# One-layer decoder trunk on one core: the low parts of the MLP's and the last gate's weight chunks come from an accumulating transfer instead of a VectorE subtraction

## The chip, the cores and the metric

The kernel runs on one core of one Trainium2 chip. The metric is the device time of one execution in microseconds (us). The profile is of one execution, with times counted from the first instruction of the span. Engines are called by the profile's names: PE is TensorE (PEld its weight loads), DVE is VectorE, ACT is ScalarE, POOL is GpSimd, and SP is the engine whose queue issues most transfers.

## What is computed

One layer on a 512 x 1024 residual stream `x`, all in float32:

```
h = RMSNorm(x)
[conv_a | conv_b | q | k | v | pool | gates] = h @ W_in
mix = W_out( sum_b sigmoid(gate_b) * y_b ); x += RMSNorm(mix)     # y: conv, attention, pooling
x += RMSNorm( squared-ReLU MLP( RMSNorm(x) ) )                    # 1024 -> 4096 -> 1024
x += sigmoid(x @ W_pg) * (p @ W_pe)
```

The change touches the weights of the last two lines: the MLP's two matrices and the gate `W_pg`.

## The kernel before

**Products.** Activations lie with features on the 128 partitions and the 512 tokens along the free dimension. A float32 product is made of three fast ones: each operand is split into a high part `h`, rounded to the fast product's type, and an exact rest `l`, and `mm3` (lines 153 to 155 of the kernel's text) adds h·h, h·l and l·h in one PSUM bank. In the profile L153 and L155 read `wh` and `wl` against the high part of the moving operand, and L154 reads `wh` against its low part.

**Weights.** All matrices are packed into 142 chunks of 128 x 1024 floats (512 KB), in the order in which they are used. Chunks 62 to 69 are `W_out`, 70 to 133 the MLP in four quarters of the hidden width (eight chunks of its first matrix, then eight of its second), 134 to 141 the last gate. A chunk serves one output tile: 8 steps over the inner dimension (kt) of three products, 24 products in all. The class `Weights` loads a chunk on SP's queue into one of 3 raw buffers (L75), `split` (L86) makes the high part on ACT (L89, a cast) and the low part on DVE (L93, raw minus high), into one of 8 pairs of buffers in the part that matters here; `get` asks for chunks ahead, as far as buffers and `W.limit` allow. A pair comes free when PE has done the last product of the chunk that held it, eight chunks earlier.

**Order.** Each engine runs its own list in order. A scheduler makes the lists from the program's text by a model of times; in the stretches marked `manual_schedule` PE's own instructions keep the order of the text. `W.pin` with `keep_in_program_order` ties an instruction to its place behind the one that is written before it on the same engine: `side_by_side_halves` (L865) uses it for the four chunks (74 to 77, later 138 to 141) that it asks for after 15 steps of products.

**The two norms at the MLP's start.** `W_out`'s last five tiles and the MLP's first four (chunks 70 to 73, `side_by_side_halves`) are multiplied by halves of the tokens, so that the norm of one half runs while the other half is multiplied. For each half, `residual_half` (L842) lets PE sum squares (L210), DVE and POOL make the reciprocal root (L200, L202), PE spread it (L215) and ACT copy it to `mB` (L845). Then DVE scales the eight tiles `mix` (L850), POOL adds them to `x` (L851), and ACT and DVE split the scaled `x` into `xgh` and `xgl` (`mul_split`, L148 and L149), which are the operand of the MLP's first matrix. The sums of squares for the second norm (`x1sum`) are gathered on the way. Its reciprocal root, needed only after the first matrix, goes through DRAM: `rstd_dma` (L219) copies a row of sums (ACT, L223), and four transfers follow one another in POOL's queue: `d1` (L226), `c4` (L228), after a power on POOL `d2` (L230), and `rB` (L232). `hidden` (L892) needs `rB` to make the operand `sh`, `sl` of the second matrix. The same scheme by halves stands at the MLP's end, with `f`, `fsum`, `fB` and `x2h`, `x2l` in place of `mix`, `msum`, `mB`, `xgh` and `xgl`.

Of the kernel before, what the change touches and what calls it, by code (L numbers as in the profile page):

```python
# [13 lines left out]

# the work of the first half in order, by the letters of the table
ORDER = [dict(A="conv", Q="qk", V="v", P="pool", p="pool out", a="attention out", c="conv gates")[c]
         for c in "QAVPAAQQQppppcAaaaaccc"]
# shares of TensorE's time given to the background work during projections and gates
RATE_IN, RATE_GATE = 0.6, 0.907
# of the steps of background work, how many are taken from the first queue for one from the second  # L20
TURNS = 2
# steps to wait for the sums of a norm: a head's, the last head's, LayerNorm's
NORM_LAG, WAIT_SUB, WAIT_LN = 10, 4, 8
# start: tiles of x loaded before the second chunk; chunks split before x is normalized; normalized
# tiles of x before the next chunks; products that bring up the array's clock
X_BEFORE_W1, W_EARLY, XN_BEFORE_W3, XN_BEFORE_W4, N_WARM = 3, 2, 2, 7, 8
# products of a half before the other half's sums, and before they are spread; chunks split after that
PACE_SUM, PACE_SPREAD, W_AHEAD = 8, 15, 3
# output tiles multiplied side by side before those by halves
N_SIDE = 3  # L30
# slots: raw chunks, split chunks, activations, logits, tiles of norms, q and k
N_RAW, N_SPLIT, N_ACT, N_LOGIT, N_NORM, N_QK = 3, 3, 32, 6, 3, 10
TCARGS = dict(schedule_with_timeline_sim=True)
P = 128
# [10 lines left out]

# columns of the packed small parameters
G_PRE_MIX, G_POST_MIX, G_PRE_MLP, G_POST_MLP = 0, 8, 16, 24
# [9 lines left out]
class Weights:  # L57
    """Streams the packed weight chunks in order: a load and a split of each
    chunk into its rounded high part and the exact rest."""

# [25 lines left out]
    def split(self, c, sl=slice(0, 1024), parts="hl"):  # L86
        src, (wh, wl) = self.raw[c][:, sl], self.tiles[c]
        if "h" in parts:
            i = self.nc.scalar.copy(out=wh[:, sl], in_=src)  # L89
            if self.pin:  # L90
                self.tc.keep_in_program_order(i)
        if "l" in parts:
            i = self.nc.vector.tensor_tensor(out=wl[:, sl], in0=src, in1=wh[:, sl].bitcast(F32), op=ALU.subtract)  # L93
            if self.pin:
                self.tc.keep_in_program_order(i)
# [15 lines left out]
def block_kernel(ctx: ExitStack, tc: tile.TileContext, xT, pT, wts, pool_w, par, rel_bias, onehot, out):  # L111
# [15 lines left out]

    # tiles that wait for a long chain have slots of their own: slots of a tag are
    # given out in order, so they would hold up all that comes after them
    BUFS = {"a": N_ACT, "lg": N_LOGIT, "bias": 2, "norm": N_NORM}  # L130
# [15 lines left out]
    def mul_split(h, l, src, scale=1.0):  # L146
        """h + l = src * scale, h rounded to the fast product's operand."""
        nc.scalar.activation(out=h, in_=src, func=AF.Copy, scale=scale)  # L148
        nc.vector.scalar_tensor_tensor(out=l, in0=src, scalar=scale, in1=h.bitcast(F32),  # L149
                                       op0=ALU.mult, op1=ALU.subtract)  # L150
# [5 lines left out]

# [1 line left out]
    start = ExitStack()  # L158
# [28 lines left out]
    nc.vector.memset(neghalf, -0.5)  # L187
    # products whose result nobody reads, so that the array's clock is up when the data comes
    warm = bank("at")
# [5 lines left out]

# [1 line left out]
    def rstd_from(ssq, inv_n, n, name):  # L197
        """[P, n] sums -> (sum * inv_n + eps) ** -0.5"""
        c = small(n, name + "c")
        nc.vector.tensor_scalar(out=c, in0=ssq, scalar1=inv_n, scalar2=EPS, op0=ALU.mult, op1=ALU.add)  # L200
        r = small(n, name + "r")
        nc.gpsimd.tensor_tensor(out=r, in0=c, in1=neghalf[:, 0:n], op=ALU.pow)  # L202
        return r

    def rstd_steps(sq, lo, n, inv_n, got, tag="at"):
        """column sums of sq[:, lo:lo+128n] to rstd, the same on every partition, in PSUM: a step
        for the sums and one that spreads them and hands them to got"""
        b = bank(tag)
        for j in range(n):
            nc.tensor.matmul(out=b[:, j:j + 1], lhsT=sq[:, lo + j * P:lo + (j + 1) * P], rhs=ones_col,  # L210
                             start=True, stop=True)
        r = rstd_from(b[:, 0:n], inv_n, n, "pe")
        yield
        for j in range(n):
            nc.tensor.matmul(out=b[:, j * P:(j + 1) * P], lhsT=r[:, j:j + 1].to_broadcast([P, P]),  # L215
                             rhs=ident, start=True, stop=True)
        got(b[:, 0:n * P])
# [16 lines left out]

    # ---- background streams: steps for DVE between the products, each step
    # yielding its cost in us, or None when it can't go on yet ----
    class Stream:
# [3 lines left out]
        def step(self):  # L241
            """one step; its cost, or None when the stream is blocked or over"""
            try:
                return next(self.gen)
            except StopIteration:
                self.over = True
                return None
# [41 lines left out]

# [1 line left out]
    LEFT, RIGHT = slice(0, 512), slice(512, 1024)  # L291
# [73 lines left out]

# [1 line left out]
    lam_t = cp.tile([P, 8], F32, name="lam_t")  # L367
# [11 lines left out]

    # sigmoid(z) = (1 + tanh(z / 2)) / 2, so that one table serves exp and the gates;  # L380
    # the factor 1/2 goes where a scale is applied anyway
    nc.vector.tensor_scalar(out=pcol(DW_W, 4 * CW), in0=pcol(DW_W, 4 * CW), scalar1=0.5, scalar2=None, op0=ALU.mult)
# [9 lines left out]
    nc.sync.dma_start(out=rel_d, in_=rel_r)  # L392
    # row r of a head's bias is its row of distances moved by r
    rep_d = dr.tile([NH, P, 640], F32, name="rep_d")
# [3 lines left out]

# [1 line left out]
    def project(n, evac, side_by_side=False):  # L400
        """n output tiles of the combined projection"""
        bs = []
        if side_by_side:
            cs = [next_chunk() for _ in range(n)]
            bs = [bank() for _ in range(n)]
            for kt in range(KT):
                for (wh, wl), b in zip(cs, bs):
                    mm3(b, wh[:, kt * P:(kt + 1) * P], wl[:, kt * P:(kt + 1) * P], *xn[kt], kt == 0, kt == KT - 1)
        else:
            for _ in range(n):  # L410
                wh, wl = next_chunk()
                bs.append(bank())
                for kt in range(KT):
                    mm3(bs[-1], wh[:, kt * P:(kt + 1) * P], wl[:, kt * P:(kt + 1) * P], *xn[kt], kt == 0, kt == KT - 1)
                    tick(0.65 * RATE_IN)
        return evac(bs)
# [3 lines left out]
    def evac_qk(bs):  # L420
        """q and k of a head's two maps, stacked so that a product over 128 rows holds two of the
        three terms: high q twice against high and low k; and low q where the high k lies"""
        qb, kb = bs
# [25 lines left out]
    def attention():  # L449
# [37 lines left out]
        def transpose(i):  # L487
            # keys of all blocks up to this pair of query blocks on the partitions
            qb = i % 4
# [196 lines left out]

# [1 line left out]
    merged = [None] * KT  # L688
# [78 lines left out]

    # ---- output projection; its last tiles by token halves, so that the norm
    # of one half runs while the other half is multiplied ----
    x_t = []  # L770
# [13 lines left out]
    class Paced:  # L784
        """the steps of a norm, set between the products of the other half"""

# [14 lines left out]
    def split_output(src, evac, done):  # L801
        """8 output tiles of a product over 8 kt: some side by side, the others by halves."""
        W.limit = chunk[0] + KT + 3
# [38 lines left out]
    def residual_half(hf, src, ssum, rB, xs, use):  # L842
        """xs += src * rstd of the half, and what uses the sum"""
        sl = HALVES[hf]
# [18 lines left out]

# [1 line left out]
    def side_by_side_halves(src, done):  # L865
# [67 lines left out]

# [1 line left out]
    proj = []  # L935
# [36 lines left out]
def _layout(inp):  # L972
# [7 lines left out]
    def tiles(w):  # L980
        """[K, M] -> [M/128][128, K/128, 128]"""
        k, m = w.shape
# [89 lines left out]
```

## Time and profile before

| | |
|---|---|
| time, median of 3 runs | 867.05 us (865.79 to 867.57) |
| span of the profiled execution | 864.5 us |
| PE busy | 848.3 us (98%) |
| DVE busy | 512.3 us (59%) |
| ACT busy | 352.5 us (41%) |
| POOL busy | 50.4 us (6%) |
| moved by DMA | 89.38 MB, mean 103 GB/s |

The profiled execution's span is 2.55 us below the median of the three runs, which hold what lies around the span as well; a sum made on the trace is added to the median as it stands. Busy is the time in which an engine had an instruction under way; the rows below show single instructions, groups of them, or stretches of the span.

### The profile page before, as it was taken

What the parts mean: (1) busy time and instruction counts of PE and PEld (TensorE: products, weight loads), DVE (VectorE), ACT (ScalarE), POOL (GpSimd) and SP (SyncE); (2) the same over time, 40 slices, a digit from 0 to 9 for tenths busy, and PEclk for the clock granted to TensorE, in tenths of its full rate; (3) what the DMA queues carried; (4) which work ended last, traced back from release to release, by engine and by line L of the source; (5) the groups of instructions that cost most, each with busy time, mean ns of one, the idle gap of its engine ahead of it and who ended that gap; (6) DMA issues with size and microseconds to landing.
All of it is one profiled execution on the core that took longest, in us unless ns stands there. A gap on an engine that the chain in (4) does not pass through costs nothing.

```text
span 864.5 us, 10723 instructions
## 1 busy us (share of the span) xinstructions
PE 848.3 (98%) x4202; PEld 707.9 (82%) x4202; DVE 512.3 (59%) x803; ACT 352.5 (41%) x568; POOL 50.4 (6%) x85
## 2 busy tenths in 40 slices
PE   9979999999999999999999999999999999999998
PEld 6767888777778888888999778888888888889987
DVE  5749659965559996658368453344344434425682
ACT  6625435464443323553454354342124313425341
POOL 2100000010000000000033100000000000000420
PEclk9989999999999999999999999999999999999999
DMA  8353222121122222255201614222222222212311
GB/s 296 122 194 114 106 98 98 68 91 54 69 74 74 96 99 96 76 191 204 91 27 53 204 49 146 98 98 97 99 98 98 97 90 88 99 65 75 122 50 74
DMA packets 28127, 89.38 MB, mean 103 GB/s; under 512 B 3272, under 2 KB 3656, under 8 KB 28076
## 3 DMA queue, kind: packets, MB, share of 16 engines
q1 hardware_dynamic: 27260, 86.32, 28.6%
q0 software_dynamic: 816, 2.37, 0.7%
q8 instruction: 33, 0.54, 0.2%
q14 instruction: 18, 0.15, 0.1%
HBM read 84.47 MB, written 5.52 MB: 104 GB/s over the span
## 4 chain that ended last, share of the span: by engine, by line
PE 86%; DVE 5%; DMA 4%; issue 3%; ACT 1%; POOL 1%; SPq 0%; DVEq 0%; ACTq 0%; POOLq 0%
PE mm L153 19%; PE mm L155 19%; PE mm L154 19%; PE at L153 8%; PE at L154 8%; PE at L155 8%; DMA raw<-in_wts_dram 2%; DVE f L850 1%; PE at L462 1%; PE at L215 1%; POOL x L851 1%; PE at L210 1%; DVE mix L850 1%; PE at L460 1%; PE at L493 1%
## 5 line engine op out<-in xcount | busy, mean ns | idle before, releaser
L89 ACT CAST wh<-raw 128x1024 fp32r<-128x1024 f32 (+1 forms) x144 | 148.6, 1038 | 334.5 <-PE mm L154 151.0
L93 DVE TENSOR_TENSOR wl<-raw,wh 128x1024 fp32r<-128x1024 f32 (+1 forms) x144 | 173.4, 1209 | 104.6 <-ACT wh L89 104.3
L155 PE MATMUL mm<-xnh,wl 128*128 128x512 f32 x352 | 138.6, 394 | 0.1
L153 PE MATMUL mm<-xnh,wh 128*128 128x512 f32 x352 | 137.9, 394 | 0.0
L154 PE MATMUL mm<-xnl,wh 128*128 128x512 f32 x352 | 137.8, 392 | 0.0
L582 DVE SCALAR_TENSOR_TENSOR acc<-u,par_sb,acc 128x512 f32<-128x512 f32 x116 | 82.2, 748 | 0.1
L153 PEld LDWEIGHTS mm<-xnh,wh 128*128 128x128 f32 x352 | 66.1, 188 | 15.7 <-issue 1.0
L155 PEld LDWEIGHTS mm<-xnh,wl 128*128 128x128 f32 x352 | 66.1, 188 | 15.0 <-issue 0.8
L154 PEld LDWEIGHTS mm<-xnl,wh 128*128 128x128 f32 x352 | 66.1, 188 | 13.8 <-DVE xnl L149 0.4
L153 PE MATMUL mm<-sh,wh 128*128 128x512 f32 (+1 forms) x152 | 54.4, 358 | 0.0
L154 PE MATMUL mm<-sl,wh 128*128 128x512 f32 (+1 forms) x152 | 54.2, 357 | 0.0
L155 PE MATMUL mm<-sh,wl 128*128 128x512 f32 (+1 forms) x152 | 54.2, 356 | 0.0
L154 PE MATMUL at<-xgl,wh 128*128 128x512 f32 (+1 forms) x144 | 52.8, 366 | 1.2 <-DVE xgl L149 1.2
L153 PE MATMUL at<-sh,wh 128*128 128x512 f32 (+1 forms) x144 | 53.4, 371 | 0.3 <-ACT sh L148 0.3
L154 PE MATMUL at<-sl,wh 128*128 128x512 f32 (+1 forms) x144 | 53.1, 369 | 0.2 <-DVE sl L149 0.2
L155 PE MATMUL at<-sh,wl 128*128 128x512 f32 (+1 forms) x144 | 52.9, 367 | 0.0
L153 PE MATMUL at<-xgh,wh 128*128 128x512 f32 (+1 forms) x144 | 52.9, 367 | 0.0
L153 PE MATMUL mm<-xgh,wh 128*128 128x512 f32 (+1 forms) x144 | 52.7, 366 | 0.0
L155 PE MATMUL at<-xgh,wl 128*128 128x512 f32 (+1 forms) x144 | 52.7, 366 | 0.0
L154 PE MATMUL mm<-xgl,wh 128*128 128x512 f32 (+1 forms) x144 | 52.6, 365 | 0.0
L155 PE MATMUL mm<-xgh,wl 128*128 128x512 f32 (+1 forms) x144 | 52.6, 365 | 0.0
L202 POOL TENSOR_TENSOR per<-pec,neghalf 128x4 f32<-128x4 f32 (+1 forms) x10 | 10.5, 1052 | 533.2 <-DVE pec L200 533.2
(247 smaller groups left out, 1583.3 us busy)
## 6 DMA issues: line engine op xcount, KB each, us to landing
raw<-in_wts_dram SPq DMA_DIRECT2D x140, 512.0 KB, 3.2
x<-in_xT_dram SPq DMA_DIRECT2D x16, 256.0 KB, 5.9
proj_d<-proj POOLq DMA_DIRECT2D x8, 256.0 KB, 3.9
proj<-proj_d SPq DMA_DIRECT2D x8, 256.0 KB, 3.7
out_dram<-pg SPq DMA_DIRECT2D x7, 256.0 KB, 2.0
rep_d<-rel_d SPq DMA_DIRECT2D x1, 1280.0 KB
raw<-in_wts_dram SPq DMA_DIRECT2D x4, 256.0 KB, 5.4
bias<-rep_d SPq DMA_DIRECT2D x4, 256.0 KB, 4.5
```

Of the source, the lines that this page charges most:

```text
L89: i = self.nc.scalar.copy(out=wh[:, sl], in_=src)
L93: i = self.nc.vector.tensor_tensor(out=wl[:, sl], in0=src, in1=wh[:, sl].bitcast(F32), op=ALU.subtract)
L153: nc.tensor.matmul(out=o, lhsT=sh, rhs=mh, start=first, stop=False)
L154: nc.tensor.matmul(out=o, lhsT=sh, rhs=ml, start=False, stop=False)
L155: nc.tensor.matmul(out=o, lhsT=sl, rhs=mh, start=False, stop=last)
L202: nc.gpsimd.tensor_tensor(out=r, in0=c, in1=neghalf[:, 0:n], op=ALU.pow)
L210: nc.tensor.matmul(out=b[:, j:j + 1], lhsT=sq[:, lo + j * P:lo + (j + 1) * P], rhs=ones_col, start=True, stop=True)
L215: nc.tensor.matmul(out=b[:, j * P:(j + 1) * P], lhsT=r[:, j:j + 1].to_broadcast([P, P]), rhs=ident, start=True, stop=True)
L460: nc.tensor.matmul(out=lg[m][:, 0:nn], lhsT=q[m][:, cols], rhs=k[m][:, 0:nn], start=True, stop=False)
L462: nc.tensor.matmul(out=lg[m][:, 0:nn], lhsT=ql[own, cols], rhs=k[m][own, 0:nn], start=False, stop=True)
L582: nc.vector.scalar_tensor_tensor(out=t, in0=u[:, k:k + S], scalar=pcol(w0 + k), in1=t, op0=ALU.mult, op1=ALU.add)
L850: nc.vector.tensor_tensor(out=src[m][:, sl], in0=src[m][:, sl], in1=rB[:, sl], op=ALU.mult)
```

## The change

From chunk 74 on (`LOW_BY_DMA = 74`: the MLP without its first four chunks, and the gate, 68 chunks) DVE no longer subtracts. ACT makes a second pass over the raw chunk and writes its negated high part into the low part's buffer (new line 95), and a transfer issued from POOL's queue then reads the chunk from DRAM once more and adds it to what stands there (new line 96). The raw buffer is free after ACT's two passes. The pin of `keep_in_program_order` still covers ACT's cast, and covers neither of the two new instructions.

```
+LOW_BY_DMA = 74
...
             i = self.nc.scalar.copy(out=wh[:, sl], in_=src)
             if self.pin:
                 self.tc.keep_in_program_order(i)
-        if "l" in parts:
+        if "l" in parts and c >= LOW_BY_DMA:
+            self.nc.scalar.activation(out=wl[:, sl], in_=src, func=AF.Copy, scale=-1.0)
+            self.nc.gpsimd.dma_start(out=wl[:, sl], in_=self.w[c][:, sl], accum_op=ALU.add)
+        elif "l" in parts:
             i = self.nc.vector.tensor_tensor(out=wl[:, sl], in0=src, in1=wh[:, sl].bitcast(F32), op=ALU.subtract)
             if self.pin:
                 self.tc.keep_in_program_order(i)
```

The scheduler's lists change with it. In the changed kernel's text a line of this part stands five lines later (L223 is L228 there, and so on). The first place is POOL's queue from the end of the MLP's first four tiles to `rB`; `wl78` is the low part of chunk 78. Before:

```order
L226 DMA d1_x1_4249<-row_585_4247 16x1x32
L228 DMA c4_586_4252<-d1_x1_4249 128x4
L202 TENSOR_TENSOR dmr_588_4256<-dmc_587_4254,neghalf_131 128x4
L230 DMA d2_x1_4250<-dmr_588_4256 128x4
L232 DMA rB_589_4259<-d2_x1_4250 128x512
```

Now:

```order
L96 DMA wl78_4296<-in_wts_dram 128x1024
L96 DMA wl79_4303<-in_wts_dram 128x1024
L96 DMA wl80_4310<-in_wts_dram 128x1024
L231 DMA d1_x1_4253<-row_585_4251 16x1x32
L96 DMA wl81_4317<-in_wts_dram 128x1024
L96 DMA wl82_4356<-in_wts_dram 128x1024
L233 DMA c4_586_4256<-d1_x1_4253 128x4
L96 DMA wl83_4395<-in_wts_dram 128x1024
L207 TENSOR_TENSOR dmr_588_4260<-dmc_587_4258,neghalf_131 128x4
L96 DMA wl84_4434<-in_wts_dram 128x1024
L235 DMA d2_x1_4254<-dmr_588_4260 128x4
L237 DMA rB_589_4263<-d2_x1_4254 128x512
```

Seven accumulating transfers now stand ahead of and between the norm's four.

The second place is ACT at the norm of the first tokens' half, up to the copy of the second half's `mB`; `xgh_520` to `xgh_526` are the high parts of tiles 4 to 7 of the operand's first half. Before, they stand 9 to 15 rows ahead of that copy:

```order
L148 ACTIVATE xgh_516_3467<-x_497_3442,par_sb_96 128x256
L148 ACTIVATE xgh_518_3469<-x_498_3444,par_sb_96 128x256
L148 ACTIVATE xgh_520_3471<-x_499_3446,par_sb_96 128x256
L148 ACTIVATE xgh_522_3473<-x_500_3448,par_sb_96 128x256
L831 ACTIVATE sq_551_3893<-at_538_3599 128x256
L836 ACTIVATE mix_509_3460<-at_538_3599,par_sb_96 128x256
L148 ACTIVATE xgh_524_3475<-x_501_3450,par_sb_96 128x256
L148 ACTIVATE xgh_526_3477<-x_502_3452,par_sb_96 128x256
```

Now, at the copy:

```order
L91 CAST wh77_4099<-raw77_4097 128x1024
L95 ACTIVATE wl77_4100<-raw77_4097 128x1024
L153 ACTIVATE xgh_520_3471<-x_499_3446,par_sb_96 128x256
L850 COPY mB_528_3479<-at_567_3966 128x256
L153 ACTIVATE xgh_522_3473<-x_500_3448,par_sb_96 128x256
L153 ACTIVATE xgh_524_3475<-x_501_3450,par_sb_96 128x256
L153 ACTIVATE xgh_526_3477<-x_502_3452,par_sb_96 128x256
L153 ACTIVATE xgh_512_3463<-x_495_3438,par_sb_96 128x256
```

The casts of chunks 75 to 77 and the negations of chunks 74 to 77 have moved from behind both halves of the norm to between the first half's tiles; three of the first half's high parts now follow the second half's `mB`.

The third place is DVE at the same copy. Before, after the first half's `xgl` were long done:

```order
L850 TENSOR_TENSOR mix_503_3454<-mix_503_3454,mB_528_3479 128x256
L850 TENSOR_TENSOR mix_504_3455<-mix_504_3455,mB_528_3479 128x256
L850 TENSOR_TENSOR mix_505_3456<-mix_505_3456,mB_528_3479 128x256
L850 TENSOR_TENSOR mix_506_3457<-mix_506_3457,mB_528_3479 128x256
L850 TENSOR_TENSOR mix_507_3458<-mix_507_3458,mB_528_3479 128x256
L850 TENSOR_TENSOR mix_508_3459<-mix_508_3459,mB_528_3479 128x256
L850 TENSOR_TENSOR mix_509_3460<-mix_509_3460,mB_528_3479 128x256
L850 TENSOR_TENSOR mix_510_3461<-mix_510_3461,mB_528_3479 128x256
L149 SCALAR_TENSOR_TENSOR xgl_513_3464<-x_495_3438,par_sb_96,xgh_512_3463 128x256
```

Now:

```order
L855 TENSOR_TENSOR mix_503_3454<-mix_503_3454,mB_528_3479 128x256
L855 TENSOR_TENSOR mix_504_3455<-mix_504_3455,mB_528_3479 128x256
L855 TENSOR_TENSOR mix_505_3456<-mix_505_3456,mB_528_3479 128x256
L855 TENSOR_TENSOR mix_506_3457<-mix_506_3457,mB_528_3479 128x256
L855 TENSOR_TENSOR mix_507_3458<-mix_507_3458,mB_528_3479 128x256
L855 TENSOR_TENSOR mix_508_3459<-mix_508_3459,mB_528_3479 128x256
L154 SCALAR_TENSOR_TENSOR xgl_523_3474<-x_500_3448,par_sb_96,xgh_522_3473 128x256
L855 TENSOR_TENSOR mix_509_3460<-mix_509_3460,mB_528_3479 128x256
L855 TENSOR_TENSOR mix_510_3461<-mix_510_3461,mB_528_3479 128x256
L154 SCALAR_TENSOR_TENSOR xgl_525_3476<-x_501_3450,par_sb_96,xgh_524_3475 128x256
L154 SCALAR_TENSOR_TENSOR xgl_527_3478<-x_502_3452,par_sb_96,xgh_526_3477 128x256
L154 SCALAR_TENSOR_TENSOR xgl_513_3464<-x_495_3438,par_sb_96,xgh_512_3463 128x256
```

The first half's `xgl_523` (tile 5) now follows six of the second half's scalings, and `xgl_525` and `xgl_527` follow all eight.

## Rows read from the trace of the kernel before

**Rows 1.** The page: the span's busy times, and the chain that ended last
```profile
PE 848.3 (98%) x4202; PEld 707.9 (82%) x4202; DVE 512.3 (59%) x803; ACT 352.5 (41%) x568; POOL 50.4 (6%) x85
PE 86%; DVE 5%; DMA 4%; issue 3%; ACT 1%; POOL 1%; SPq 0%; DVEq 0%; ACTq 0%; POOLq 0%
```
**Rows 2.** The page's groups: busy us, mean ns of one, idle before, releaser
```profile
L89 ACT CAST wh<-raw 128x1024 fp32r<-128x1024 f32 (+1 forms) x144 | 148.6, 1038 | 334.5 <-PE mm L154 151.0
L93 DVE TENSOR_TENSOR wl<-raw,wh 128x1024 fp32r<-128x1024 f32 (+1 forms) x144 | 173.4, 1209 | 104.6 <-ACT wh L89 104.3
```
**Rows 3.** DMA from 550 to 750 us: packets, MB, engines' share; issues, us to landing
```profile
q1 hardware_dynamic: 5184, 18.88, 26.8%
...
raw<-in_wts_dram SPq DMA_DIRECT2D x37, 512.0 KB, 3.2
```
**Rows 4.** Timeline of PE, 475 to 498 us: start, us, instruction, idle before
```profile
475.33 1.02 PE L221 MATMUL at<-x1sum,ones_col 128*1 128x512 f32 x2
476.27 0.50 PE L153 MATMUL at<-xgh,wh 128*128 128x512 f32 x1
...
498.18 0.50 PE L153 MATMUL at<-sh,wh 128*128 128x512 f32 x1
```
**Rows 5.** Timeline of POOL, 479 to 500 us
```profile
479.79 0.56 POOL L226 DMA_DIRECT2D d_x<-row  x1 [15.51 <-ACT row L223]
482.61 0.59 POOL L228 DMA_DIRECT2D c<-d_x  x1 [2.25 <-DMA d_x<-row]
487.42 1.03 POOL L202 TENSOR_TENSOR dmr<-dmc,neghalf 128x4 f32<-128x4 f32 x1 [4.23 <-DVE dmc L200]
488.76 0.60 POOL L230 DMA_DIRECT2D d_x<-dmr  x1 [0.30 <-POOL dmr L202]
492.78 0.55 POOL L232 DMA_DIRECT2D rB<-d_x  x1 [3.42 <-DMA d_x<-dmr]
```
**Rows 6.** Timelines of ACT and DVE: the row of sums, and the first hidden tile
```profile
478.94 0.57 ACT L223 COPY row<-at 1x512 f32<-1x512 f32 x1
...
497.49 0.63 ACT L148 ACTIVATE sh<-t 128x512 fp32r<-128x512 f32 x1
...
496.10 0.69 DVE L894 SCALAR_TENSOR_TENSOR t<-at,rB 128x512 f32<-128x512 f32 x1 [6.51 <-DMA rB<-d_x]
```
**Rows 7.** POOL's eight stores at the start: ns to issue, us to landing
```profile
L364 POOL DMA_DIRECT2D proj_d<-proj x8: 539/539/731, 17.8 to 32.8; - x8
...
DMA to landing us min/median/max: 2.7/3.9/5.3
```
**Rows 8.** Timelines of ACT and DVE at the second half's copy of mB
```profile
456.35 0.37 ACT L845 COPY mB<-at 128x256 f32<-128x256 f32 x1 [3.94 <-PE at L215]
...
456.76 6.07 DVE L850 TENSOR_TENSOR mix<-mix,mB 128x256 f32<-128x256 f32 x8 [0.71 <-ACT mB L845]
462.75 1.82 DVE L149 SCALAR_TENSOR_TENSOR xgl<-x,par_sb,xgh 128x256 fp32r<-128x256 f32 x2
```
**Rows 9.** Timeline of PE at the same place
```profile
456.07 0.36 PE L153 MATMUL mm<-xgh,wh 128*128 128x256 f32 x1
...
462.27 0.28 PE L153 MATMUL at<-xgh,wh 128*128 128x256 f32 x1
463.75 0.39 PE L154 MATMUL at<-xgl,wh 128*128 128x256 f32 x1 [1.20 <-DVE xgl L149]
```
**Rows 10.** Stretches: us, busy of PE, PEld, DVE, ACT, POOL, granted clock, DMA
```profile
441.00:456.00 15.00, 14.66 (x123) 14.45 (x122) 14.45 (x28) 9.19 (x24) 7.92 (x9) 1.00 0.07 27
800.00:813.00 13.00, 12.18 (x104) 11.97 (x102) 12.11 (x23) 5.84 (x15) 7.01 (x8) 1.00 0.57 189
...
54.00:58.00 4.00, 1.73 (x4) 1.45 (x5) 1.75 (x2) 2.83 (x4) 0.00 (x0) 0.50 0.63 201
58.00:62.00 4.00, 4.00 (x13) 3.10 (x13) 4.00 (x12) 1.43 (x2) 0.00 (x0) 0.66 0.55 183
815.00:818.00 3.00, 3.00 (x17) 3.00 (x16) 0.00 (x0) 0.00 (x0) 0.59 (x1) 0.51 0.00 0
```
**Rows 11.** Timeline of PE at the MLP's end, its two waits
```profile
814.00 0.61 PE L210 MATMUL at<-ones_col,fsum 128*128 128x1 f32 x4 [1.83 <-DVE fsum L832]
...
826.58 0.38 PE L154 MATMUL at<-x2l,wh 128*128 128x256 f32 x1 [1.18 <-DVE x2l L149]
```

More of the change, by code (lines that the diff above doesn't have):

```diff
@@ L32 @@
 N_RAW, N_SPLIT, N_ACT, N_LOGIT, N_NORM, N_QK = 3, 3, 32, 6, 3, 10
+LOW_BY_DMA = 74
 TCARGS = dict(schedule_with_timeline_sim=True)
@@ L91, in split @@
                 self.tc.keep_in_program_order(i)
-        if "l" in parts:
+        if "l" in parts and c >= LOW_BY_DMA:
+            self.nc.scalar.activation(out=wl[:, sl], in_=src, func=AF.Copy, scale=-1.0)
+            self.nc.gpsimd.dma_start(out=wl[:, sl], in_=self.w[c][:, sl], accum_op=ALU.add)
+        elif "l" in parts:
             i = self.nc.vector.tensor_tensor(out=wl[:, sl], in0=src, in1=wh[:, sl].bitcast(F32), op=ALU.subtract)
```

## The prediction

> **What bounds the kernel now.** I read the page's busy times and chain first, then the groups of the lines that the change touches, then DMA in the MLP, then the timelines of all engines at the MLP's start and end. PE is busy 98% of the span and the chain that ended last is 86% PE [rows 1], so an engine's saved work counts only where PE waits for it. The subtraction is cheap to lose: one takes 1.21 us on DVE, a cast on ACT 1.04 us, and ACT's idle time ahead of its casts is time spent waiting for PE to free a buffer [rows 2]. From 476.27 to 498.18 PE runs four chunks of the MLP at 5.48 us each without a pause [rows 4]; nothing that DVE does for the weights is late there. Where PE waits after that point and before the end, it is for norms: 1.20 us at 463.75, 1.83 at 814.00 and 1.18 at 826.58 [rows 9, 11]. One more place has no wait and no room either: the second norm's trip through DRAM. Its row of sums is copied at 478.94, the four transfers go out at 479.79, 482.61, 488.76 and 492.78 [rows 5, 6], the first hidden tile starts at 496.10, its high part is done at 497.49 + 0.63 = 498.12, and PE takes it up at 498.18 [rows 4, 6]. Every microsecond by which that trip grows is one that PE stands still.
>
> **What goes: 68 subtractions on DVE,** 68 x 1.21 = 82 us of work beside PE. By the rows none of it is what PE waits for, so I give nothing for it; at most the three waits above could shrink.
>
> **What comes in the steady part.** 68 more passes on ACT (taken at the cast's price, the same shape and engine, 0.95 us from start to start) and 68 transfers. Where a chunk is split once its buffers come free, it is ready now about 2 us later; with the second pass, the issue on POOL (about 0.6 us, as rows 5 show) and the landing it is some 8 us, and PE needs it seven chunks, 38 us, after the buffer came free. ACT has the room, and hides it. The transfer's price is the open quantity. Call A the time for which one occupies the 16 DMA engines. A plain load of the same 512 KB takes 26.8% x 200 us / 37 = 1.45 us and lands 3.2 us after its issue, so 1.75 us of that is fixed [rows 3]. An accumulating one reads what stands in the buffer as well as the source and writes once. From below A is 1.45 (the second read is free); from above I take three passes' worth, 4.35; nearest is two reads' worth, 2.9, which I choose. The DMA engines are then taken (1.45 + 2.9) / 5.48 = 79% of the time in the MLP and keep up; they stop keeping up at A = 5.48 - 1.45 = 4.03. The Trainium skill (Collectives: The Full Stack, the part on why the measured rate is seven times under the link's) says that a reducing transfer is slower than a copying one because it needs two source reads, and gives a measured ratio of 1.93; by it an estimate for A would be 2.8 and the total 0.7 us less. No run here shows it yet.
>
> **Term 1, the norm of the first tokens: +2.7 us.** The scheduler has put four negations and three casts, 7 x 0.95 = 6.7 us, on ACT before the second half's `mB`. ACT is idle 15.00 - 9.19 = 5.8 us from 441 to 456, and three `xgh` move behind the copy [rows 10], so `mB` still comes at about 456.7 [rows 8]. But DVE now makes `xgl_523` after six scalings of 6.07 / 8 = 0.76 us: 456.76 + 4.55 = 461.3 start, about 462.0 done, since one took up to 0.9 us beside POOL (1.82 for two at 462.75) [rows 8]. PE begins the sixteenth group of three products at 456.07; 17 groups take it to 462.27, 0.36 us each [rows 9]. With this and four more it is at 457.9, and there it needs tile 5. It stands till 462.0, less 0.46 us (2 x 21.9 / 96, rows 4) for two whole-tile products that the scheduler has drawn to this place (these too wait, for ACT's second-half `xgh_512`). Twelve groups follow, 4.3 us, with some 0.5 us more before `xgl_525`: the first half ends at 466.8, not at 462.27. There the old wait of 1.48 us (463.75 against 462.27) is gone, since `xgl_513` is ready by then. So the first group of tiles ends 466.8 - 463.75 = 3.1 us later; 0.46 us come back because those two products are done: +2.7.
>
> **Term 2, the second norm's trip: +16.6 us.** Let G be the end of these four tiles (475.3 before [rows 4]). Chunk 78 waits for the buffers of chunk 70, free about 1 us before G. Its cast and negation take two passes: its transfer goes out at G + 1.0. POOL issues 78, 79, 80, then `d1` behind them; `c4` behind 81 and 82; `d2` behind 83 and 84. If transfers of one queue land in turn, each of the seven costs A, and beside each runs about one raw load of 1.45, since ACT frees one raw buffer for each negation. So `d1` lands at G + 1.0 + 1.75 + 3(A + 1.45), `c4` 2(A + 1.45) later, `d2` 2(A + 1.45) later again; the power and `rB`'s own 3.3 us (492.78 to 496.10) add 3.9. The hidden tile starts at G + 6.65 + 7(A + 1.45) and its high part is done 2.0 us later, as now (498.12 - 496.10) [rows 6]. PE comes there at G + 0.9 (the sum, 475.33 to 476.27) + 21.9 - 0.46 = G + 22.4. Its stall is 7(A + 1.45) - 13.7: 16.7 us at A = 2.9, 6.6 at 1.45, 26.9 at 4.35. Before, the same sum gives nothing (496.10 is G + 20.8). I take 16.6.
>
> That the small transfers wait in turn behind the large ones is an inference. The one place where POOL's queue is filled shows eight stores issued 0.54 us apart in two bursts, landing after 2.7 to 5.3 us [rows 7], which fits it. The Trainium skill (DMA: Bandwidth & Descriptors, the section on queues, rings and completion order) states that an engine consumes the descriptors of one ring in ring order; these rows agree. If small ones passed ahead, POOL's own order would still hold them: the transfer of chunk 84 stands before `d2` and waits for chunk 76's buffers, PE's third tile after G (G + 16.9), and for two passes, so `d2` goes out at G + 19.5, lands 3.7 us later [rows 5], and with `rB` and the hidden tile PE stalls some 6.4 us. So the floor of this term is the same 6.5 by either road.
>
> **Term 3, the MLP's end: +1.5 us.** Up to eight passes of ACT (negations of 137 to 141, casts of 139 to 141, 7.6 us) now stand between 800 and 813, where ACT is idle 13.00 - 5.84 = 7.2 us [rows 10]. The squares for the last sum come 0 to 3 us later, and PE waits for the sum already [rows 11]: +1.9, and some 0.4 less at the second wait.
>
> **Term 4, the clock: +3.4 us.** Early in the span, where PE is busy for 1.73 of 4 us, its granted clock was 0.50 over 54 to 58 and still 0.66 over 58 to 62, when it had work throughout, against 1.00: up to 2.0 + 1.4 = 3.4 us lost; behind the wait of 1.83 us that ended at 814.00 it was 0.51 for 3 us, 1.5 us lost [rows 10, 11]. 0.50 is 1.2 GHz of the two levels, 1.00 is 2.4. A stall of 17 us should cost the first, and term 1's wait at most the second; I take 3.4 for both.
>
> Sum: 2.7 + 16.6 + 1.5 + 3.4 = 24.2. The profiled span of 864.5 us would become 889, and the median 867.05 + 24.2 = 891 us.
>
> **Rivals.** *The DMA engines become the bound.* If A is above 4.03, each of the 56 or so chunks after the stall comes A + 1.45 - 5.48 late, through the whole MLP. At 4.35: 2.7 + 26.9 + 56 x 0.32 + 1.5 + 3.4 = 52, 919 us; at 4.65 about 938; at 5.8 (four passes) some 144, 1011 us. Against it: 26.8% busy now leaves much room [rows 3]. For it: no row has such a transfer, and whether its adding keeps pace is unknown. *The transfer is as cheap as a plain one, or the small ones pass ahead:* 2.7 + 6.5 + 1.5 + 3.4 = 14.1, 881 us. *Faster:* the freed DVE shortens PE's waits for `xgl`, `fsum` and `x2l` (1.20 + 1.83 + 1.18 = 4.2 us [rows 9, 11]): 863 us. It needs the norm's trip to fit in G + 22.4, that is 7(A + 1.45) under 13.7, or A under 0.5, and none of terms 1 and 3. Against it: POOL's order, and L850 and L149 on DVE, not L93, fill the time before those waits [rows 8]. *No change* would need the same with waits as they were, 867 us.
>
> **How the numbers follow.** 891 as forecast (A from 2.2 to 3.8, 885 to 903): 0.55. DMA-bound: 0.22. Cheap or passing ahead, about 881: 0.17. Faster: 0.03; within 0.2%, about what a measurement of this kernel can tell from no change: 0.03. Slower is the rest, 0.94. The range runs from 878, below the cheap case, to 940, where A is 4.65; left out are the 0.06, a few hundredths of the cheap case, and the dearer half of the DMA-bound one.
>
> **What would show it.** Right: in the changed profile PE idles some 17 us before its first product of `sh`, with POOL's `d1`, `c4` and `d2` landing 9 us and more after their issue; a PE wait of 2 to 4 us near 458 on `xgl`; clock 0.5 behind the long stall; no PE wait from there to 800; `wl` transfers landing about 5 us after issue when alone. Wrong: DMA busy near 100% through the MLP and PE waiting for `wl` at every chunk (A above 4); or `d1`, `c4` and `d2` landing in 3 to 4 us as now, which takes term 2 to 6; or PE meeting `sh` without a stall, which takes away the forecast altogether.

## The result and the profile after

The changed kernel takes 893.98 us (median of four runs, 893.64 to 894.98) against 867.31 us for the kernel before beside it: a ratio of 1.0314, 95% interval 1.0298 to 1.0331. The forecast was 891. The profiled execution has a span of 892.0 us against 864.5, so 27.5 us have to be found in the trace.

First the page of the changed kernel: the busy times, and the group of the accumulating transfer's issue.

```profile
PE 854.0 (96%) x4202; PEld 713.4 (80%) x4202; DVE 433.0 (49%) x735; ACT 414.5 (46%) x636; POOL 107.8 (12%) x153
...
L96 POOL DMA_DIRECT2D wl<-in_wts_dram x68 | 58.4, 863 | 281.6 <-ACT wl L95 270.0
```

DVE lost 79 us of work against [rows 1] and ACT gained 62; PE fell from 98% to 96%. POOL's issue of an accumulating transfer takes 0.86 us, not the 0.6 that the small ones took in [rows 5].

The second view is DMA in the steady part of the MLP, 550 to 750 us (packets, MB, share of the 16 engines; the loads' issues with their us to landing), the answer to [rows 3].

```profile
q0 software_dynamic: 5651, 20.59, 55.6%
q1 hardware_dynamic: 5735, 20.87, 33.4%
...
raw<-in_wts_dram SPq DMA_DIRECT2D x39, 512.0 KB, 7.5
```

This is the price that the trace of before could not show. 20.59 MB are 39.3 transfers of 0.524 MB, so an accumulating one occupies the engines for 0.556 x 200 / 39.3 = 2.83 us; 2.9 had been taken. The plain loads beside it take 0.334 x 200 / 39.8 = 1.68 us, where [rows 3] give 0.268 x 200 / 36.0 = 1.49. Together 89% of the engines' time: they keep up.

The third view is PE's timeline at all places where it waits from the first norm on. The number in brackets is the idle time before the instruction.

```profile
459.28 0.73 PE L158 MATMUL mm<-xgh,wh 128*128 128x512 f32 x2 [0.49 <-ACT xgh L153]
462.49 0.39 PE L159 MATMUL at<-xgl,wh 128*128 128x256 f32 x1 [2.48 <-DVE xgl L154]
...
464.59 0.39 PE L159 MATMUL at<-xgl,wh 128*128 128x256 f32 x1 [0.40 <-DVE xgl L154]
...
520.10 0.79 PE L158 MATMUL at<-sh,wh 128*128 128x512 f32 x1 [18.48 <-ACT sh L153]
...
833.33 0.39 PE L159 MATMUL at<-x2l,wh 128*128 128x256 f32 x1 [0.43 <-DVE x2l L154]
840.31 1.01 PE L215 MATMUL at<-ones_col,fsum 128*128 128x1 f32 x4 [3.97 <-DVE fsum L837]
...
854.28 0.39 PE L159 MATMUL at<-x2l,wh 128*128 128x256 f32 x1 [0.95 <-DVE x2l L154]
```

One wait stands out: 18.48 us before the first product of `sh`, which in [rows 4] PE met without a pause. Around the first norm it waits 0.49 + 2.48 + 0.40 = 3.37 us where [rows 9] show 1.20; at the MLP's end 0.43 + 3.97 + 0.95 = 5.35 where [rows 11] show 3.01 (waits under 0.4 us are left out of both). From 521 to 832 us PE has no wait.

Behind the long waits the granted clock is at its lower level. The stretches (us, busy time of PE, PEld, DVE, ACT, POOL, granted clock, DMA share, GB/s):

```profile
508.00:513.00 5.00, 0.00 (x0) 0.00 (x0) 0.00 (x0) 0.00 (x0) 0.18 (x1) 0.50 0.70 133
520.00:524.00 4.00, 3.90 (x9) 2.75 (x10) 2.57 (x4) 1.30 (x3) 0.00 (x0) 0.50 0.00 0
524.00:528.00 4.00, 4.00 (x15) 3.23 (x14) 1.31 (x3) 2.52 (x4) 0.00 (x0) 0.76 0.00 0
840.00:843.00 3.00, 2.69 (x12) 2.69 (x13) 1.51 (x5) 1.49 (x5) 1.14 (x2) 0.50 1.07 262
843.00:847.00 4.00, 4.00 (x22) 4.00 (x21) 0.00 (x0) 0.10 (x1) 0.00 (x0) 0.53 0.79 157
```

The clock was already at 0.50 (1.2 GHz) while PE stood idle at 508, and PE worked at it until about 526: 3.90 x 0.50 + 4.00 x 0.24 = 2.9 us lost. At the end 2.69 x 0.50 + 4.00 x 0.47 = 3.2 us, against 1.5 before [rows 10]. The sum: 2.2 (first norm) + 18.5 (second norm) + 2.3 (end) + 2.9 + 1.7 (clock) = 27.6, against 27.5 us of span.

Why `sh` comes late is read from POOL's timeline, the answer to [rows 5], and from the landing times of the four small transfers (the last number of the second fence's lines).

```profile
484.05 0.86 POOL L96 DMA_DIRECT2D wl<-in_wts_dram  x1 [1.04 <-ACT wl L95]
484.60 0.83 POOL L231 DMA_DIRECT2D d_x<-row  x1
...
493.43 0.85 POOL L96 DMA_DIRECT2D wl<-in_wts_dram  x1 [6.14 <-ACT wl L95]
498.15 0.58 POOL L233 DMA_DIRECT2D c<-d_x  x1 [3.87 <-DMA d_x<-row]
...
506.71 0.89 POOL L96 DMA_DIRECT2D wl<-in_wts_dram  x1
507.33 0.85 POOL L235 DMA_DIRECT2D d_x<-dmr  x1
513.08 0.56 POOL L237 DMA_DIRECT2D rB<-d_x  x1 [4.91 <-DMA d_x<-dmr]
```

```profile
rB<-d_x POOLq DMA_DIRECT2D x1, 256.0 KB, 4.8
d_x<-row POOLq DMA_DIRECT2D x1, 2.0 KB, 13.0
c<-d_x POOLq DMA_DIRECT2D x1, 2.0 KB, 7.3
d_x<-dmr POOLq DMA_DIRECT2D x1, 2.0 KB, 5.5
```

The same four in the kernel before:

```profile
rB<-d_x POOLq DMA_DIRECT2D x1, 256.0 KB, 3.3
d_x<-row POOLq DMA_DIRECT2D x1, 2.0 KB, 2.5
c<-d_x POOLq DMA_DIRECT2D x1, 2.0 KB, 3.8
d_x<-dmr POOLq DMA_DIRECT2D x1, 2.0 KB, 3.7
```

In the order `d1`, `c4`, `d2`, `rB` that is 2.5 + 3.8 + 3.7 + 3.3 = 13.3 us together; now they take 13.0 + 7.3 + 5.5 + 4.8 = 30.6. These 17 us are most of the stall. The other 1.4 us is that `d1` goes out later: 17.0 us before PE comes to `sh` (at 501.62) instead of 18.4, because ACT copies the row of sums only at 483.66, behind six passes over chunks.

Whether the small transfers wait in turn behind the large ones, which the prediction could only infer, can be read from the trace. These are the landing times of the accumulating transfers issued at 484.05, 493.43 and 506.71, each the last one ahead of a small transfer in POOL's queue:

```profile
wl<-in_wts_dram POOLq DMA_DIRECT2D x1, 512.0 KB, 13.2
wl<-in_wts_dram POOLq DMA_DIRECT2D x1, 512.0 KB, 11.8
wl<-in_wts_dram POOLq DMA_DIRECT2D x1, 512.0 KB, 5.9
```

They land at 497.25, 505.23 and 512.6. `d1`, `c4` and `d2` land at 497.6, 505.45 and 512.8, each 0.2 to 0.4 us behind the large one ahead of it. So all three wait in turn.

### The profile page after: what moved, and what is told of

It is laid out like the page before. It is cut to its first block, busy times and chain, and to the rows that moved or that the text cites. A ratio compares the mean times of both kernels' runs of the same rounds, so it can differ in the third digit from the quotient of the medians.

```text
span 892.0 us, 10859 instructions
## 1 busy us (share of the span) xinstructions
PE 854.0 (96%) x4202; PEld 713.4 (80%) x4202; DVE 433.0 (49%) x735; ACT 414.5 (46%) x636; POOL 107.8 (12%) x153
## 4 chain that ended last, share of the span: by engine, by line
PE 87%; DMA 5%; DVE 4%; ACT 2%; issue 1%; POOL 0%; SPq 0%; ACTq 0%; POOLq 0%; DVEq 0%
PE mm L158 19%; PE mm L160 19%; PE mm L159 19%; PE at L159 8%; PE at L158 8%; PE at L160 8%; DMA raw<-in_wts_dram 2%; DMA d_x<-row 1%; DVE f L855 1%; DVE mix L855 1%; PE at L467 1%; PE at L220 1%; PE at L215 1%; DMA d_x<-dmr 1%; PE at L465 1%
## 5 line engine op out<-in xcount | busy, mean ns | idle before, releaser
L98 DVE TENSOR_TENSOR wl<-raw,wh 128x1024 fp32r<-128x1024 f32 (+1 forms) x76 | 90.5, 1194 | 67.9 <-ACT wh L91 67.6
L96 POOL DMA_DIRECT2D wl<-in_wts_dram x68 | 58.4, 863 | 281.6 <-ACT wl L95 270.0
L95 ACT ACTIVATE wl<-raw 128x1024 fp32r<-128x1024 f32 x68 | 71.8, 1055 | 0.0
L158 PE MATMUL at<-sh,wh 128*128 128x512 f32 (+1 forms) x144 | 53.8, 375 | 18.5 <-ACT sh L153 18.5
L154 DVE SCALAR_TENSOR_TENSOR sl<-t,sh 128x512 fp32r<-128x512 f32 x32 | 22.2, 692 | 69.3 <-ACT sh L153 69.3
```

The costliest lines, as they stand in the source:

```text
L95: self.nc.scalar.activation(out=wl[:, sl], in_=src, func=AF.Copy, scale=-1.0)
L96: self.nc.gpsimd.dma_start(out=wl[:, sl], in_=self.w[c][:, sl], accum_op=ALU.add)
L158: nc.tensor.matmul(out=o, lhsT=sh, rhs=mh, start=first, stop=False)
```

## The experiments

**Theory:** what is lost is lost at the two norms and at the MLP's end, most of it because the second norm's four small transfers stand among accumulating ones on POOL and in its queue; everything between is hidden. **Rivals:** a small cost of each of the 68 transfers everywhere; the load of the DMA engines whatever the queue; the lost hold on program order. Each experiment starts from the changed kernel.

**Only the middle.** Chunks 86 to 133, clear of both norms.

```diff
-        if "l" in parts and c >= LOW_BY_DMA:
+        if "l" in parts and 86 <= c < 134:
```

> Only the 48 chunks 86 to 133, from after the second norm's trip to the end of the MLP, get their low part by the accumulating transfer; all others by DVE as before. Theory (the loss sits at the norms, the steady part is hidden): 867, within 1.5 of before, no PE wait over 0.5 us between 500 and 800. Rival 1 (each transfer and negation costs a little everywhere, 26.7 us / 68 = 0.39 each): 867 + 48 x 0.39 = 886. Rival 2 (DVE's 58 us of freed work pays once the norms are left alone): below 864.

866.88 us, ratio 1.0000 (0.9988 to 1.0013). The stretch from 530 to 800 us, first this kernel, then the kernel before:

```profile
530.00:800.00 270.00, 270.00 (x1262) 225.03 (x1261) 56.57 (x86) 130.96 (x163) 39.96 (x46) 1.00 0.81 189
```
```profile
530.00:800.00 270.00, 270.00 (x1265) 225.12 (x1264) 108.93 (x129) 87.56 (x116) 0.72 (x1) 1.00 0.26 93
```

DVE's busy time is halved, ACT's is half as much again, the DMA engines go from 26% to 81%, and PE is busy 270 of 270 us in both. Both rivals fall: 48 transfers cost nothing, and 58 us of freed DVE bring nothing.

**Only the start.** Chunks 74 to 85 (the condition reads `74 <= c < 86`).

> Only the 12 chunks 74 to 85, at the start of the MLP, get the accumulating transfer. Theory: the first norm's reordering (2.4), the stall of 18.6 before the first product of sh and the half clock behind it (2.9) all stay, 867 + 24 = 891. Rival (cost in proportion to the number of transfers, 0.39 each): 867 + 12 x 0.39 = 872.

888.85 us, ratio 1.0257 (1.0236 to 1.0278). Twelve transfers of 68 bring 22.1 us of the loss, where the rival allowed 5. It is 2 us under the theory's number; the last section returns to that.

**The second norm first.** All 68 transfers stay, and POOL's order is fixed: `d1`, `c4`, the power, `d2` and `rB` ahead of the accumulating transfers of chunks 78 and up.

```diff
-            self.nc.gpsimd.dma_start(out=wl[:, sl], in_=self.w[c][:, sl], accum_op=ALU.add)
+            (self.tc.keep_in_program_order if 78 <= c <= 90 else id)(self.nc.gpsimd.dma_start(out=wl[:, sl], in_=self.w[c][:, sl], accum_op=ALU.add))
...
-        nc.gpsimd.dma_start(out=d1, in_=row)
+        tc.keep_in_program_order(nc.gpsimd.dma_start(out=d1, in_=row))
```

(and so for `c4`, the power, `d2` and `rB`.)

> All 68 transfers stay as in the changed kernel, but POOL's order is fixed by hand: d1, c4, the power, d2 and rB of the second norm stand ahead of the accumulating transfers of chunks 78 and up. Theory (place in POOL's queue): the trip is as short as before, rB some 13 us after d1's issue, no stall of 18.6 before sh and no 2.9 us of half clock; chunks 79 and 80 then come a little late, some 3 us in all: 894 - 21.5 + 3 = 875. Rival (DMA load, or the second pass of ACT): both are as in the changed kernel, so 890 to 894.

879.35 us, ratio 1.0150 (1.0127 to 1.0174): 12.6 us lost, so 14.1 of the 26.7 are back. The landing times, then PE's waits:

```profile
rB<-d_x POOLq DMA_DIRECT2D x1, 256.0 KB, 5.5
d_x<-row POOLq DMA_DIRECT2D x1, 2.0 KB, 3.9
c<-d_x POOLq DMA_DIRECT2D x1, 2.0 KB, 4.0
d_x<-dmr POOLq DMA_DIRECT2D x1, 2.0 KB, 2.0
```
```profile
506.57 0.80 PE L158 MATMUL at<-sh,wh 128*128 128x512 f32 x1 [2.73 <-ACT sh L153]
...
510.78 0.80 PE L160 MATMUL mm<-sh,wl 128*128 128x512 f32 x1 [1.41 <-DMA wl<-in_wts_dram]
```

15.4 us in all, near the 13.3 of before, and the stall is 2.73 us in place of 18.48: with as many transfers and passes of ACT, the order on POOL makes the difference. This order also keeps the accumulating transfers off the DMA engines during the trip (their share is 0.60 over 486 to 499, where the changed kernel has 1.05 over 484 to 500), so this run does not part the place in the queue from the load; the landings in turn above do. What lies over the expectation is mostly the clock, which I had thought would stay up. In the profiled execution, at 881.7 us the slowest of the four, it is at 0.62, 0.50 and 0.70 over 505 to 510, 510 to 514 and 514 to 518, with 2.80, 3.22 and 4.00 us of PE's work, so 3.9 us are lost behind these two short waits.

**A plain copy.** The transfer of each chunk copies in place of adding (the subtraction is left out); order and count are unchanged.

```diff
-            self.nc.gpsimd.dma_start(out=wl[:, sl], in_=self.w[c][:, sl], accum_op=ALU.add)
+            self.nc.gpsimd.dma_start(out=wl[:, sl], in_=self.w[c][:, sl])
```

> The changed kernel with a plain copy of the chunk into wl in place of the accumulating one (the low part is then the chunk itself, the subtraction is left out); order and number of instructions are the same. Theory: the stall before sh is 7(A + 1.45) plus a constant, and with A 1.45 in place of 2.8 to 2.9 it falls by 7 x 1.4 = 10 us, from 18.6 to 8 or 9; 884 in all. Rival (only the order on POOL and ACT counts, not how long a transfer takes): 18.6 as now, 894.

882.84 us, ratio 1.0188 (1.0166 to 1.0209). POOL's queue from 550 to 750 us, and the end of the stall:

```profile
q0 software_dynamic: 5513, 20.09, 28.0%
```
```profile
511.72 0.80 PE L158 MATMUL at<-sh,wh 128*128 128x512 f32 x1 [8.74 <-ACT sh L153]
```

20.09 MB are 38.3 transfers: 1.46 us each, so the adding costs a factor of 2.83 / 1.46 = 1.94. The Trainium skill (Collectives: The Full Stack, the part on why the measured rate is seven times under the link's) gives 1.93 for a reducing against a copying collective; this case agrees. The stall falls from 18.48 to 8.74 us, by 9.7 where 7 x (2.83 - 1.46) = 9.6: in the total the transfer's time enters seven times, as the prediction had it. In the parts it does not: `d1` lands 6.3 us sooner, `c4` 2.1 and `d2` 1.5 us after their issue, where three, two and two transfers would give 4.1, 2.7 and 2.7.

**The seven alone by DVE.** Chunks 78 to 84 as before the change (the condition gets `and not 78 <= c <= 84`), the 61 others by transfer.

> The changed kernel, but the seven chunks 78 to 84, whose transfers stood ahead of the second norm's, get their low part by DVE as before; 61 of the 68 transfers stay. Theory (those seven are the stall): no stall before sh; what is left is the first norm's reordering (2.4) and the MLP's end (2.6 and 1.7 of half clock): 867 + 6.7 = 874. Rival (about 3 us of stall came from the four transfers 74 to 77 or from the passes on ACT, as some stayed when the norm went first): 877.

872.46 us, ratio 1.0067 (1.0050 to 1.0084). PE's first product of `sh`:

```profile
502.51 0.39 PE L158 MATMUL at<-sh,wh 128*128 128x512 f32 x1
```

The row has no idle time in brackets: nothing stands before it. Seven transfers of 68, with their negations, make the stall. The 5.9 us left are the first norm and the end.

**Only the last gate.** Chunks 134 to 141 (`c >= 134`).

> Only the eight chunks 134 to 141, those of the last gate, get the accumulating transfer. Theory (their passes on ACT stand ahead of the squares of the last sum): PE's wait for the sum is 4.1 in place of 2.0, a half clock of 6.8 us in place of 3.4 follows: 867 + 2.5 + 1.7 = 871. Rival (what is late at the end comes from the MLP's chunks before, whose transfers here are gone): 867.

869.81 us, ratio 1.0039 (1.0026 to 1.0052), 3.2 us, with the same wait for the sum as in the changed kernel:

```profile
817.66 1.02 PE L215 MATMUL at<-ones_col,fsum 128*128 128x1 f32 x4 [3.98 <-DVE fsum L837]
```

The eight own transfers of the gate suffice for it; the rival's 867 is outside the interval. With the run before, the first norm's share is 5.9 - 3.2 = 2.7 us.

**The hold on program order given back.** The negation and the transfer are held wherever the subtraction was.

```diff
-            self.nc.scalar.activation(out=wl[:, sl], in_=src, func=AF.Copy, scale=-1.0)
-            self.nc.gpsimd.dma_start(out=wl[:, sl], in_=self.w[c][:, sl], accum_op=ALU.add)
+            (self.tc.keep_in_program_order if self.pin else id)(self.nc.scalar.activation(out=wl[:, sl], in_=src, func=AF.Copy, scale=-1.0))
+            (self.tc.keep_in_program_order if self.pin else id)(self.nc.gpsimd.dma_start(out=wl[:, sl], in_=self.w[c][:, sl], accum_op=ALU.add))
```

> All 68 chunks as in the changed kernel, but the negation and the accumulating transfer are held in program order wherever the subtraction was. Theory: the first norm's reordering goes (-2.4), but the transfers of chunks 74 to 77 now go out behind that norm's second half, and 78 to 80 behind them, so that more of them than before stand between the row of sums and d1: the stall grows from 18.6 to about 26; 896. Rival (the lost pin is what the change costs): 870 to 875.

888.40 us, ratio 1.0258 (1.0238 to 1.0278), and the stall:

```profile
520.47 0.79 PE L158 MATMUL at<-sh,wh 128*128 128x512 f32 x1 [21.60 <-ACT sh L153]
```

Neither number was met. The rival falls: 21.8 us are still lost, so the hold alone gives 4.9 back of 26.7. The theory's direction holds for the stall (it grows, by 3.1 us), but not its size, and it had not counted that the end heals too: PE's waits there are 1.83 and 1.18 us, as before the change.

**The small transfers on ACT's queue.** `d1`, `c4`, `d2` and `rB` by `nc.scalar.dma_start`; the accumulating ones stay on POOL.

> The changed kernel with d1, c4, d2 and rB of the second norm issued from ACT's queue in place of POOL's; the accumulating transfers stay on POOL. Theory (a small transfer is late because large ones stand before it in its own queue): d1 lands within 4.5 us of its issue although accumulating transfers are under way, where it took 13. Rival (the 16 engines are loaded, whatever the queue): 9 us or more. In both the trip now stands in ACT's order among casts that wait for buffers, so the stall stays near 14 and the total near 889.

888.84 us, ratio 1.0254 (1.0234 to 1.0273), stall 12.82 us: `c4` goes out only at 497.02, since it stands in ACT's order among casts that wait. `d1` was issued at 486.12, and the profile has no landing time for it; but the only two packets of ACT's queue (q10) in the next twelve microseconds lie in 489 to 490 and in 490 to 491, which the first two lines show. The third is `c4`'s landing time.

```profile
q10 hardware_dynamic: 1, 0.00, 0.6%
```
```profile
q10 hardware_dynamic: 1, 0.00, 0.1%
```
```profile
c<-d_x ACTq DMA_DIRECT2D x1, 2.0 KB, 7.9
```

So `d1` took at most 4.9 us in a queue of its own, against 13.0 behind three accumulating transfers, with the DMA engines equally full (1.01 against 1.05 over 484 to 500). It is also carried differently, in 2 packets here and in 32 in POOL's queue, so this pair alone does not show the place; with the landings in turn it does. The Trainium skill (DMA: Bandwidth & Descriptors, the section on queues, rings and completion order) has an engine consume one ring's descriptors in ring order, and `d1`, `c4` and `d2` in the changed kernel agree. But `c4` took 7.9 us in its own queue, no less than the 7.3 in POOL's: here it is 144 packets and not 32, with the DMA engines full (1.06 over 500 to 507). Which of the two makes the 7.9 was not tried. In POOL's queue its delay is the place, since it lands 0.2 us behind the large transfer; a queue of its own does not by itself take the delay away.

**The middle and the end, held.** Chunks 86 to 141, with the hold of the run before last (`c >= 86`).

> The 56 chunks 86 to 141 get the accumulating transfer, and where the subtraction was held in program order the negation and the transfer are too (at the end of the MLP). Theory (the end's loss in the eight-chunk run, 3.2 us, came from passes that slipped ahead of the last sum's squares on ACT): the waits at the end are 2.0 and 1.3 us as before, 867 within 1.5. Rival (the loss there came from the transfers' load on the DMA engines): 870.

867.24 us, ratio 1.0004 (0.9992 to 1.0015), the wait for the sum as in [rows 11]:

```profile
815.61 0.61 PE L215 MATMUL at<-ones_col,fsum 128*128 128x1 f32 x4 [1.84 <-DVE fsum L837]
```

With the gate's transfers still there, the end costs nothing. The hold moves these transfers behind the sum too, so the run alone does not part ACT's order from the load. ACT's timeline in the changed kernel does: the squares of the last sum stand behind passes that slipped ahead of them, and ACT is busy 4.00 of the 4.00 us from 836 to 840, so it waits for no transfer there.

```profile
835.62 1.04 ACT L95 ACTIVATE wl<-raw 128x1024 fp32r<-128x1024 f32 x1
...
836.87 0.40 ACT L836 ACTIVATE sq<-f 128x256 f32<-128x256 f32 x1
...
838.11 1.05 ACT L95 ACTIVATE wl<-raw 128x1024 fp32r<-128x1024 f32 x1
...
839.37 0.40 ACT L836 ACTIVATE sq<-f 128x256 f32<-128x256 f32 x1
```

**The second norm first, and the negations held.** All 68 transfers, with the order on POOL of the run that put the second norm first, and with the negation, but not the transfer, held wherever the subtraction was.

> All 68 transfers, the second norm's four small ones first in POOL's order, and the negations held in program order. Theory: against the run with the norm first alone (879.4) the first norm's reordering (2.7) and the MLP's end (3.2) go, and some 3 us come back since the transfers of chunks 74 to 77 now stand just ahead of d1: 876. Rival (the pinned negations delay the row of sums and the trip by all of that): 880 or more.

874.58 us, ratio 1.0094 (1.0080 to 1.0108).

```profile
506.15 0.80 PE L158 MATMUL at<-sh,wh 128*128 128x512 f32 x1 [7.45 <-ACT sh L153]
```

The first norm's and the end's losses go; what stays is a stall of 7.45 us before `sh` and the low clock behind it, since four accumulating transfers now stand ahead of `d1`, which lands after 7.9 us, 0.3 us behind the last of them. No kernel here beats the kernel before: PE sets its time, and the change takes nothing from PE.

## Why the prediction held, step by step

- **The steady part at nothing, the freed DVE at nothing.** Right, shown by the run of the middle alone.
- **The transfer's price, 2.9 of 1.45 to 4.35.** 2.83, under the 4.03 at which the DMA engines would have become the bound. That rival's threshold was not tried. The plain load's 1.45 divides by the 37 issues of the stretch; its bytes are those of 36.0 transfers, so it was 1.49, and it is 1.68 beside the accumulating ones.
- **Term 1, +2.7.** 2.2 in the profile, 2.7 in the runs. DVE made `xgl_523` at 461.50 (forecast 461.3), PE took it up at 462.49 and had waited 0.49 and 2.48 us. This loss goes when the negation is held in order.
- **Term 2, +16.6.** 18.5, the largest miss. The road was right, seven transfers landing in turn with the small ones between them. So was their sum: from chunk 78's issue to chunk 84's landing the trace has 32.4 us (480.26 to 512.6), the prediction 1.75 + 7 x 4.35 = 32.2. That it fits so closely is luck: the first takes 9.0 us where 6.1 were taken, the other six 3.9 each where 4.35 were. What the term had too small is `rB`, 4.8 us in place of 3.3: in POOL's queue it takes 4.7 to 5.7 us in the five profiles where a large transfer goes out right behind it, and 3.3 to 4.0 in the five where none is near. The sign that `d1`, `c4` and `d2` would land 9 us and more after their issue is met by `d1` alone (13.0); `c4` and `d2` take 7.3 and 5.5, since part of the wait for the large ones ahead was over when they went out.
- **Term 3, +1.5.** 2.3 of waits; by cause right (ACT's passes ahead of the squares), too small: the wait for the sum grew by 2.1 (1.9 forecast), the second one shrank by 0.2 only (1.18 to 0.95, 0.4 forecast), and one of 0.43, not forecast, came 7 us ahead of the sum.
- **Term 4, +3.4.** 2.9 behind the stall, near the forecast, and 1.7 more at the end, which the term left out: a wait of 3.97 us there was followed by a longer stretch at the low clock than the 1.83 before.
- **Rivals.** "Cheap, or passing ahead", 881, is what the plain copy gives (882.8); its other half, a small transfer that passes the large ones, is not what a shared queue did. The band beside the chances is added up wrongly: A from 2.2 to 3.8 gives 886 to 898 by the prediction's own sum, not 885 to 903.

## What to carry to other kernels

Work moved to an idle engine's queue is free only if nothing short that others wait for lives in that queue. List the short chains that pass through it, count what can stand ahead of each link, and set the order there by hand or leave that stretch out: seven transfers of 68 made four fifths of this loss (26.7 us against 5.9 without them). And a replacement must take over the hold on program order of what it replaces, on each engine that it now uses.

## What the hardware showed beside this

A wait of the same length did not always bring the low clock. PE waits 1.83 us for the last sum in the run of the middle and 1.74 in the run of the start; the stretch that holds the end of this wait and what follows, first for the middle, then for the start:

```profile
814.00:818.00 4.00, 3.37 (x18) 3.37 (x19) 0.58 (x2) 0.63 (x2) 0.71 (x1) 0.67 0.22 67
```
```profile
836.00:840.00 4.00, 2.26 (x19) 2.05 (x19) 1.58 (x5) 1.40 (x4) 0.71 (x1) 1.00 0.40 117
```

The granted clock fell to 0.67 on the mean in the one and stayed at 1.00 in the other, where it had also been low some 315 us earlier, behind the stall. This fits the run of the start being under its number: it lost none of the 1.5 us that the kernel before loses there (its stall, 19.32 us, was longer than the changed kernel's). Behind a wait of 1.74 to 1.84 us for this sum the clock fell, to 0.66 or 0.67 over 4 or 5 us, in all three profiles without a long stall before `sh` (the kernel before, the middle, the middle and the end held), and stayed at 1.00 in all three with one (the start, the hold given back, the last run). But each is one execution, and the executions of the kernel before differ among themselves, with a mean granted clock from 0.991 to 0.997, so chance is not excluded. What decides it stays open. Second, the loads slowed to a landing of 7.5 us from 3.2 in the steady part and PE never noticed; a load's latency says little while the buffers ahead of it are full.
